# Two wide products, then two narrow ones: the order of a column block's matmuls in a split-precision stream

## The chip, the cores and the metric

The kernel runs on one core of a Trainium2 chip. The metric is the device time in microseconds of one execution: 2563.12 us, the median of three runs that lie between 2562.52 and 2567.24 us.

## The reference

The computation is a small decoder trunk in float32, with one sequence of 256 tokens and a width of 2048. There are two layers. The first mixes tokens with a Mamba-2 state-space block, the second with a short gated convolution. Each is followed by a gated feed-forward network with a convolution of its own (hidden width 5632), and a root-mean-square norm ends it. Nearly all of the arithmetic is in the dense products by weight matrices:

```python
h = rms_norm(x, mix_norm_w[i])
x = x + mixer(h)                      # ssd_mixer (i = 0), short_conv_mixer (i = 1)
h = rms_norm(x, ffn_norm_w[i])
hu = causal_dwconv(h @ w_up, conv_w, conv_b)
g, v = jnp.split(hu, 2, axis=-1)
x = x + (silu(g) * v) @ w_down
...
return rms_norm(x, final_norm_w)
```

## The kernel before

**Split products.** TensorE takes operands in a shortened float32 form (`F32R` in the code), which drops low bits. To get more precise results the kernel splits each operand in two: a high half, which is the value rounded to that form, and a low half, which is what rounding left over. A product of weights and activations is then high by high, plus high weights by low activations, plus low weights by high activations. For the activations both halves lie side by side in one tile `hl`: 256 columns (the tokens) high, 256 columns low. For the weights they are two tiles, `wh` and `wl`.

**Units of weights.** Weights come in units of two blocks of 128 rows (`KU = 2`) by 512 columns. A unit is loaded by one DMA on SyncE's queue into a `raw` tile (line 267; four buffers). ScalarE casts it into `wh` (line 287), and VectorE subtracts to get `wl` (line 288); both have four buffers (`WB = 4`). A plan lists all units in the order of use, and `weight_unit` (line 298) hands out the next one after it has had up to three further ones loaded and split.

**Streams.** `stream` (line 308) multiplies a slice of 512 weight columns with all of an activation. The result, transposed, is 512 rows by 256 tokens, kept as four column blocks `t` of 128 weight columns each, two to a PSUM tile `pts[t // 2]`. For each unit, and in it for each column block `t` and each of the two row blocks `k`, the weights' 128 x 128 block is the stationary operand, and the activation streams past it:

- a *wide* product (line 334): high weights by the whole `hl` row block, 512 columns. The high-by-high sum falls in the first 256 columns of the PSUM tile, the high-by-low sum in the last 256.
- a *narrow* product (line 335): low weights by the high half of `hl`, 256 columns, added to the first 256 columns of the same place.

Each of them needs its own stationary block, so a weight load on TensorE (PEld in the profile) precedes every matmul. The code issues them in the order wide k=0, narrow k=0, wide k=1, narrow k=1, and then takes the next column block. A unit has eight wide and eight narrow products.

Some streams (`one` set: the state-space block's B, C and x inputs) put the high and low activation sums in the same 256 columns. They have two products of 256 columns (lines 331 and 332) in place of the wide one. The very first stream (`before` set) is interleaved by hand with the start of the kernel, and its instructions are kept in the program's order by `put = pin`. All others leave the order to the scheduler: the program's order is the priority, and the scheduler estimates by a simulation of its own when an instruction is ready, and lets a later one go first where it is not.

At the end of a stream `evac` is called for each of the two PSUM tiles: ScalarE and VectorE add the two sums, scale, convolve or add to the residual. There are three such PSUM tiles, so one of the next stream's is free at once.

The last feed-forward's down projection doesn't go through `stream`. It keeps tokens in rows (lines 858 to 860): three products of 512 columns each, with activations as the stationary operand and weights streaming past.

Of the kernel before, what the change touches and what calls it, by code (L numbers as in the profile page):

```python
# [16 lines left out]
P = 128  # L17
T = 256
# [14 lines left out]
KU = 2  # L33
# [6 lines left out]
def trunk_kernel(ctx, tc, a, out):  # L40
    nc = tc.nc
    mm = nc.tensor.matmul
# [18 lines left out]
    def uid(s):  # L61
        n_id[0] += 1
        return f"{s}_{n_id[0]}"
# [11 lines left out]
    start = ExitStack()  # L75
# [49 lines left out]
    for name, r in rows:  # L125
        base[name] = at
        lo = 0
        while lo < r.shape[0]:
            i, off = divmod(at, P)
            n = min(P - off, r.shape[0] - lo)  # L130
# [146 lines left out]
    def load_unit():  # L277
        i = len(units)
        if i == len(raws):
            load_raw()  # L280
        raw, raws[i] = raws[i], None
        wh = wpool.tile([P, KU, COLS], F32R, tag="wh", name=uid("wh"))
        wl = wpool.tile([P, KU, COLS], F32R, tag="wl", name=uid("wl"))
        units.append((wh, wl))

        def half(ks, put):
            put(nc.scalar.copy(wh[:, ks, :], raw[:, ks, :]))  # L287
            put(tt(  # L288
                out=wl[:, ks, :], in0=raw[:, ks, :], in1=wh[:, ks, :].bitcast(F32),
                op=ALU.subtract,  # L290
            ))

        if i == 0:
            return half
        with tc.high_priority(0 if i < NKD // KU else None):
            half(slice(0, KU), pin if i < NKD // KU + 2 else lambda ins: ins)

    def weight_unit(c0, kc, ahead=WB - 1):

        i = taken[0]  # L300
        assert plan[i][1:] == (c0, kc), (plan[i], c0, kc)
        taken[0] += 1
        while len(units) < min(i + ahead + 1, len(plan)):
            load_unit()
        got, units[i] = units[i], None
        return got

    def stream(c0, hls, kcs, evac, one=False, before=None):

        pts = [psm.tile([P, 2, 512], F32, tag="main", name=uid("main")) for _ in range(2)]
        n = len(kcs)
        put = (lambda ins: ins) if before is None else pin
        for u in range(0, n, KU):
            order = [(t, k) for t in range(4) for k in range(KU)]
            if before is not None and u == 0:
                before(0)
                order.sort(key=lambda tk: tk[1])  # L320
            wh, wl = weight_unit(c0, kcs[u], WB - 1 if before is None else 0)
            for at, (t, k) in enumerate(order):
                if before is not None and at == (0 if u else 2) and u + KU < n:
                    before(u // KU + 1)
                i = u + k
                o = pts[t // 2][:, t % 2, :]
                hl = hls[i // 2][:, i % 2, :]
                lw = slice(t * P, (t + 1) * P)
                first, last = i == 0, i == n - 1
                if one:  # L330
                    put(mm(o[:, 0:T], wh[:, k, lw], hl[:, 0:T], start=first, stop=False))  # L331
                    put(mm(o[:, 0:T], wh[:, k, lw], hl[:, T : 2 * T], start=False, stop=False))  # L332
                else:
                    put(mm(o, wh[:, k, lw], hl, start=first, stop=False))  # L334
                put(mm(o[:, 0:T], wl[:, k, lw], hl[:, 0:T], start=False, stop=last))  # L335
        if before is not None:
            before(n // KU)
        if taken[0] < len(plan):
            while len(units) < min(taken[0] + WB - 1, len(plan)):
                load_unit()  # L340
        for p in range(2):
            evac(p, pts[p])
# [62 lines left out]
    first = {}  # L405
# [50 lines left out]
    def bc_stream(g, o, before=None):  # L456

        res = []

        def evac(p, pt):  # L460
            k0 = DI // P + o * NG + g + 2 * p
            s = scaled(pt, first["r0"], True)
            y = conv(s, W_SSD, "ssdw", NCX, k0, "ssdb", "bc", bcpool)
            act(y, y, AF.Silu)
            res.append(y)

        stream(2 * DI + o * NG * DS + g * DS, xhl, range(NKD), evac, True, before)
        return res
# [101 lines left out]
    def xs_stream(g):  # L570
        res = [None, None]

        def evac(p, pt):
            y = conv(scaled(pt, r0, True), W_SSD, "ssdw", NCX, g * 4 + 2 * p, "ssdb", "xs", xspool)
            act(y, y, AF.Silu)
            res[p] = y

        stream(DI + g * GC, xhl, range(NKD), evac, True)
        return res

    def z_stream(g):
        res = [None, None]

        def evac(p, pt):
            q = pair_sum(pt)
            z = pair_tmp("z", sp)
            tt(out=z, in0=q, in1=rep2(r0), op=ALU.mult)
            act(z, z, AF.Silu)
            res[p] = z

        stream(g * GC, xhl, range(NKD), evac)
        return res
# [174 lines left out]
    for part in range(2):  # L767
        hid = ffn_part(0, part, xhl, r)
        last = part == 1
# [43 lines left out]
    for c in range(2):  # L813
        for q in range(4):
            ps = aux()
            for j in range(4):
                k = 4 * q + j
# [22 lines left out]
    for part in range(2):  # L840
        lo, hi = FPARTS[part]
        hid = ffn_part(1, part, xhl, r)
        n = hi - lo
        for cg in range(D // COLS):
# [17 lines left out]
            def evac(c):  # L862
                x = xtok[c][:, cols]
                tt(out=x, in0=pt[:, c, :], in1=x, op=ALU.add)  # L864
                if part == 1:
                    junk = tmp.tile([P, 512], F32, tag="tp", name=uid("tp"))
                    act(junk, x, AF.Square, accum_out=ss[:, c, cg : cg + 1])
                    tt(out=x, in0=x, in1=fin[:, cols], op=ALU.mult)
                if end:
                    finish(c)  # L870
# [42 lines left out]
```

## Time and profile before

| | |
|---|---|
| median of the runs | 2563.12 us |
| the profiled execution's own time | 2563.32 us |
| its span, first to last instruction | 2561.5 us |
| mean granted TensorE clock | 0.998 |
| TensorE matmuls | 15101, busy 99% of the span |
| TensorE weight loads | 15101, busy 87% |
| VectorE, ScalarE | busy 70% and 52% |
| DMA | 478.76 MB, mean 187 GB/s |

The busy time of an engine is the time in which at least one of its instructions is marked as running. TensorE's matmuls overlap in the marks: each is shown from its start to a modelled end, and the next starts before that. The sum of the groups' busy times is therefore larger than the span, and the distance from one matmul's start to the next is what it costs. The rows of the timeline show start, length, engine, line of the kernel, operation, tiles written and read, the shape of the stationary and of the moving operand, and a count of instructions that were merged into the row. In the rows of groups the figure behind the last bar is the time in which the engine stood idle just before such an instruction, and whom it waited for.

### The profile page before, as it was taken

The numbers are of one execution on the slowest core, as the hardware profiler recorded it, in microseconds if no ns is written. First come the engines' busy times: TensorE is split into PE (matmuls) and PEld (weight loads), VectorE is DVE, ScalarE is ACT, GpSimd is POOL, SyncE is SP. The second block draws the span as 40 slices with busy tenths as digits, with TensorE's granted clock in tenths as the row PEclk, the third lists the DMA queues.
The fourth block names the chain that finished last, engine by engine and source line by source line (L and its number), as shares of the span: only waits on it lengthen the run. The fifth ranks groups of instructions, "written<-read, shape, count | busy, mean of one in ns | idle before, by whom it ended". The sixth has DMA issues, their size and how long they took to land.

```text
span 2561.5 us, 38324 instructions
## 1 busy us (share of the span) xinstructions
PE 2544.6 (99%) x15101; PEld 2235.2 (87%) x15101; DVE 1790.2 (70%) x2601; ACT 1321.5 (52%) x1630; POOL 1.1 (0%) x8
## 2 busy tenths in 40 slices
PE   9999999999999999999999999999999999999998
PEld 9999998998888888888888888888888888888886
DVE  7888876788677776557776666666677774577765
ACT  5565643566555554345554444444555553455543
POOL 0000000000000000000000000000000000000000
PEclk9999999999999999999999999999999999999999
DMA  7666655665666665666665666666566666666664
GB/s 229 175 184 193 182 176 188 189 182 172 198 183 191 190 188 181 193 188 183 193 190 181 193 186 185 185 197 189 174 183 187 189 197 190 193 186 188 189 192 145
DMA packets 255737, 478.76 MB, mean 187 GB/s; under 512 B 17668, under 2 KB 29124, under 8 KB 255428
## 3 DMA queue, kind: packets, MB, share of 16 engines
q1 hardware_dynamic: 254643, 474.13, 61.3%
q8 instruction: 118, 1.93, 0.3%
q10 hardware_dynamic: 912, 2.18, 0.2%
q14 instruction: 64, 0.52, 0.1%
HBM read 474.09 MB, written 2.16 MB: 186 GB/s over the span
## 4 chain that ended last, share of the span: by engine, by line
PE 98%; DVE 1%; ACT 1%; DMA 0%; issue 0%; SPq 0%; DVEq 0%; ACTq 0%
PE main L334 50%; PE main L335 29%; PE main L331 3%; PE main L332 3%; PE main L858 3%; PE main L859 3%; PE main L860 3%; PE aux L649 1%; DVE wl L288 0%; PE aux L657 0%; DMA bias_bc<-in_ssd_dt_bias_dram 0%; PE aux L513 0%; PE aux L630 0%; DMA raw<-in_ssd_w_in_dram 0%; ACT wh L287 0%; PE aux L187 0%
## 5 line engine op out<-in xcount | busy, mean ns | idle before, releaser
L334 PE MATMUL main<-hl,wh 128*128 128x512 f32 x5568 | 1944.9, 396 | 0.2 <-DVE hl L218 0.2
L335 PE MATMUL main<-hl,wl 128*128 128x256 f32 x6336 | 1749.2, 281 | 1.8 <-DVE wl L288 1.8
L288 DVE TENSOR_TENSOR wl<-raw,wh 128x1024 fp32r<-128x1024 f32 (+1 forms) x881 | 1072.6, 1221 | 702.2 <-ACT wh L287 701.6
L287 ACT CAST wh<-raw 128x1024 fp32r<-128x1024 f32 (+1 forms) x881 | 920.8, 1048 | 1067.7 <-PE main L334 735.2
L334 PEld LDWEIGHTS main<-hl,wh 128*128 128x128 f32 x5568 | 1034.8, 188 | 236.7 <-issue 2.0
L335 PEld LDWEIGHTS main<-hl,wl 128*128 128x128 f32 x6336 | 1196.9, 189 | 17.6 <-DVE wl L288 2.7
L331 PE MATMUL main<-hl,wh 128*128 128x256 f32 x768 | 219.5, 287 | 2.5 <-DVE tp L354 1.3
L332 PE MATMUL main<-hl,wh 128*128 128x256 f32 x768 | 218.6, 285 | 0.0
L331 PEld LDWEIGHTS main<-hl,wh 128*128 128x128 f32 x768 | 148.2, 193 | 4.0 <-issue 2.0
L332 PEld LDWEIGHTS main<-hl,wh 128*128 128x128 f32 x768 | 148.3, 193 | 1.5 <-issue 1.1
L858 PE MATMUL main<-wh,hl 128*128 128x512 f32 x352 | 137.5, 391 | 0.8 <-DVE xtok L864 0.8
L859 PE MATMUL main<-wl,hl 128*128 128x512 f32 x352 | 137.4, 390 | 0.0
L860 PE MATMUL main<-wh,hl 128*128 128x512 f32 x352 | 137.0, 389 | 0.0
L370 DVE SCALAR_TENSOR_TENSOR tp<-tp,prm,tp 128x255 f32<-128x255 f32 x208 | 90.6, 477 | 0.0
L346 ACT COPY tp<-main 128x512 f32<-128x512 f32 x128 | 74.3, 580 | 26.0 <-PE main L335 26.0
L348 DVE TENSOR_TENSOR tp<-main,tp 128x512 f32<-128x512 f32 x128 | 87.4, 683 | 0.0
L858 PEld LDWEIGHTS main<-wh,hl 128*128 128x128 f32 x352 | 66.1, 188 | 15.3 <-DVE xtok L864 1.2
L860 PEld LDWEIGHTS main<-wh,hl 128*128 128x128 f32 x352 | 66.1, 188 | 14.2
L859 PEld LDWEIGHTS main<-wl,hl 128*128 128x128 f32 x352 | 66.1, 188 | 13.6
L370 DVE SCALAR_TENSOR_TENSOR g<-tp,prm,g 128x254 f32<-128x254 f32 (+1 forms) x176 | 74.6, 477 | 0.1
L368 ACT ACTIVATE g<-tp,prm,prm 128x256 f32<-128x256 f32 x88 | 48.2, 596 | 38.0 <-DVE tp L357 38.0
L357 DVE TENSOR_TENSOR tp<-tp,rrow 128x512 f32<-128x512 f32 x96 | 66.0, 688 | 1.8
(134 smaller groups left out, 966.9 us busy)
## 6 DMA issues: line engine op xcount, KB each, us to landing
raw<-in_ffn_w_up_dram SPq DMA_DIRECT2D x352, 512.0 KB, 3.7
raw<-in_ffn_w_down_dram SPq DMA_DIRECT2D x176, 512.0 KB, 4.1
raw<-in_ssd_w_in_dram SPq DMA_DIRECT2D x159, 512.0 KB, 4.5
raw<-in_sc_w_in_dram SPq DMA_DIRECT2D x96, 512.0 KB, 4.1
raw<-in_ssd_w_out_dram SPq DMA_DIRECT2D x64, 512.0 KB, 4.2
raw<-in_sc_w_out_dram SPq DMA_DIRECT2D x32, 512.0 KB, 4.2
cbc<-cs_d SPq DMA_DIRECT2D x32, 256.0 KB, 5.1
xt<-in_x_dram SPq DMA_DIRECT2D x8, 256.0 KB, 7.4
```

Source lines behind the costliest of these rows:

```text
L287: put(nc.scalar.copy(wh[:, ks, :], raw[:, ks, :]))
L288: put(tt(out=wl[:, ks, :], in0=raw[:, ks, :], in1=wh[:, ks, :].bitcast(F32), op=ALU.subtract,))
L331: put(mm(o[:, 0:T], wh[:, k, lw], hl[:, 0:T], start=first, stop=False))
L332: put(mm(o[:, 0:T], wh[:, k, lw], hl[:, T : 2 * T], start=False, stop=False))
L334: put(mm(o, wh[:, k, lw], hl, start=first, stop=False))
L335: put(mm(o[:, 0:T], wl[:, k, lw], hl[:, 0:T], start=False, stop=last))
L346: nc.scalar.copy(pb, pt[:, :, T : 2 * T])
L348: tt(out=s, in0=pt[:, :, 0:T], in1=pb, op=ALU.add)
L370: stt(out=y[:, j, d:T], in0=s[:, j, 0 : T - d], scalar=pcol(wname, (width - 1 - d) * nk + k0 + j), in1=y[:, j, d:T], op0=ALU.mult, op1=ALU ...
L858: mm(pt[:, c, :], hi_, wh[:, k, :], start=(i == 0), stop=False)
L859: mm(pt[:, c, :], hi_, wl[:, k, :], start=False, stop=False)
L860: mm(pt[:, c, :], lo_, wh[:, k, :], start=False, stop=(i == n - 1))
```

## The change

Within a unit, a column block now issues the products of both row blocks with the high weights first, and then both with the low weights: wide k=0, wide k=1, narrow k=0, narrow k=1. For streams with `one` set it is four products by high weights and then the two by low weights. The narrow product becomes a small function `low`. The first stream keeps the old order. Number, operands and flags of the matmuls are the same, with the accumulation's `stop` on the last narrow product as before, and the scheduler still has the last word on the order. The last down projection is not touched.

```diff
             wh, wl = weight_unit(c0, kcs[u], WB - 1 if before is None else 0)
+
+            def low(t, k):
+                i = u + k
+                put(mm(
+                    pts[t // 2][:, t % 2, 0:T], wl[:, k, t * P : (t + 1) * P],
+                    hls[i // 2][:, i % 2, 0:T], start=False, stop=(i == n - 1),
+                ))
+
             for at, (t, k) in enumerate(order):
...
-                first, last = i == 0, i == n - 1
+                first = i == 0
                 if one:
                     put(mm(o[:, 0:T], wh[:, k, lw], hl[:, 0:T], start=first, stop=False))
                     put(mm(o[:, 0:T], wh[:, k, lw], hl[:, T : 2 * T], start=False, stop=False))
                 else:
                     put(mm(o, wh[:, k, lw], hl, start=first, stop=False))
-                put(mm(o[:, 0:T], wl[:, k, lw], hl[:, 0:T], start=False, stop=last))
+                if before is not None:
+                    low(t, k)
+                elif k == KU - 1:
+                    for q in range(KU):
+                        low(t, q)
```

## The prediction

> **What bounds the kernel now.** I read the page first: the busy table, the chain of waits, the groups. Then the waits of TensorE alone, and last the order and distance of its instructions in time, since the change is one of order.
>
> ```profile
> span 2561.5 us, 38324 instructions
> PE 2544.6 (99%) x15101; PEld 2235.2 (87%) x15101; DVE 1790.2 (70%) x2601; ACT 1321.5 (52%) x1630; POOL 1.1 (0%) x8
> PE 98%; DVE 1%; ACT 1%; DMA 0%; issue 0%; SPq 0%; DVEq 0%; ACTq 0%
> L334 PE MATMUL main<-hl,wh 128*128 128x512 f32 x5568 | 1944.9, 396 | 0.2 <-DVE hl L218 0.2
> L335 PE MATMUL main<-hl,wl 128*128 128x256 f32 x6336 | 1749.2, 281 | 1.8 <-DVE wl L288 1.8
> L287 ACT CAST wh<-raw 128x1024 fp32r<-128x1024 f32 (+1 forms) x881 | 920.8, 1048 | 1067.7 <-PE main L334 735.2
> L288 DVE TENSOR_TENSOR wl<-raw,wh 128x1024 fp32r<-128x1024 f32 (+1 forms) x881 | 1072.6, 1221 | 702.2 <-ACT wh L287 701.6
> L334 PEld LDWEIGHTS main<-hl,wh 128*128 128x128 f32 x5568 | 1034.8, 188 | 236.7 <-issue 2.0
> ```
>
> The chain is TensorE for 98% of the span, and its idle time at the two lines is 2.0 us in all. ScalarE and VectorE, which split the weights, stand idle for over 700 us each while TensorE is behind. So the time is the sum of the distances between matmul starts, and only that matters here. The durations of 396 and 281 ns are no use for it: one pair of them is 677 ns, and the next pair starts after half of that. I take distances from start to start.
>
> ```profile
> L334 PE MATMUL main<-hl,wh 128*128 128x512 f32 x3925 | 1367.8, 396 | 0.0
> L335 PE MATMUL main<-hl,wl 128*128 128x256 f32 x3924 | 1080.6, 280 | 0.0
> L818 PE MATMUL aux<-ident,x 128*128 128x128 f32 x32 | 4.3, 272 | 0.0
> ```
>
> These are the groups of TensorE in the stretch from 700 to 2080 us, which is nothing but wide-narrow streams and some 56 small matmuls. 1380 us less about 6 us for those, by 3925 pairs, is 0.350 us for a wide and a narrow product. Two pairs, which is what the change reorders, take 0.700 us.
>
> **The distance isn't one number.** Here are two stretches of strict alternation, each by its first and last wide product (from the timeline) and the row that counts them.
>
> ```profile
> 361.64 0.40 PE L335 MATMUL main<-hl,wl 128*128 128x256 f32 x2
> 361.88 0.40 PE L334 MATMUL main<-hl,wh 128*128 128x512 f32 x1
> ...
> 374.71 0.39 PE L334 MATMUL main<-hl,wh 128*128 128x512 f32 x1
> L334 PE MATMUL main<-hl,wh x38: 392/394/400, 361.9 to 374.7; 128*128 128x512 f32 x38
> ...
> 384.32 0.40 PE L335 MATMUL main<-hl,wl 128*128 128x256 f32 x2
> 384.56 0.40 PE L334 MATMUL main<-hl,wh 128*128 128x512 f32 x1
> ...
> 397.63 0.40 PE L334 MATMUL main<-hl,wh 128*128 128x512 f32 x1
> L334 PE MATMUL main<-hl,wh x38: 395/398/403, 384.6 to 397.6; 128*128 128x512 f32 x38
> ```
>
> 38 starts are 37 distances. The first stretch gives 12.83 / 37 = 0.3468 us a pair, the second 13.07 / 37 = 0.3532, with the same instructions in the same order and no idle time. TensorE holds one step or the other for dozens of pairs. Two pairs cost 0.6935 in the fast step and 0.7065 in the slow one; the mean of 0.700 is about half of each. What flips it is seen where the order is broken, since the scheduler already leaves strict alternation at some unit boundaries:
>
> ```profile
> 1210.19 0.28 PE L335 MATMUL main<-hl,wl 128*128 128x256 f32 x1
> 1210.31 0.62 PE L334 MATMUL main<-hl,wh 128*128 128x512 f32 x2
> 1210.77 0.28 PE L335 MATMUL main<-hl,wl 128*128 128x256 f32 x1
> ...
> 1211.23 0.40 PE L334 MATMUL main<-hl,wh 128*128 128x512 f32 x1
> 1211.47 0.28 PE L335 MATMUL main<-hl,wl 128*128 128x256 f32 x1
> ...
> 1212.29 0.40 PE L334 MATMUL main<-hl,wh 128*128 128x512 f32 x1
> ...
> 1213.24 0.40 PE L335 MATMUL main<-hl,wl 128*128 128x256 f32 x2
> 1213.47 0.40 PE L334 MATMUL main<-hl,wh 128*128 128x512 f32 x1
> 1213.71 0.28 PE L335 MATMUL main<-hl,wl 128*128 128x256 f32 x1
> ```
>
> Two wide products in a row take 0.46 us (1210.31 to 1210.77), and the three pairs from 1211.23 to 1212.29 take 1.06 us, which is the slow step of 0.353. Two narrow ones in a row take 0.23 us (1213.24 to 1213.47), and the wide one behind them 0.24 us. A doubled product by itself costs nothing that shows, but it changes the step that follows. The change puts one at every place.
>
> **The change part by part.** No instruction is added or taken away, no DMA moves, and nothing passes another queue. In the 5568 wide products of line 334, all in streams that the change touches, two and two become a group of wide, wide, narrow, narrow: 5568 / 2 = 2784 groups. Each nanosecond of a group is 2.8 us of the kernel.
>
> *The group.* Of its four distances two are of a kind that before hardly has (wide to wide, narrow to narrow), and two stay (wide to narrow, narrow to wide). For the new kind I use stretches of one width alone.
>
> ```profile
> L858 PE MATMUL main<-wh,hl x59: 389/389/392, 2160.2 to 2199.8; 128*128 128x512 f32 x59
> ...
> 310.50 0.28 PE L332 MATMUL main<-hl,wh 128*128 128x256 f32 x1
> 310.62 0.28 PE L335 MATMUL main<-hl,wl 128*128 128x256 f32 x1
> 310.74 0.28 PE L331 MATMUL main<-hl,wh 128*128 128x256 f32 x1
> 310.86 0.28 PE L332 MATMUL main<-hl,wh 128*128 128x256 f32 x1
> ```
>
> In the last down projection, wide products alone, line 858 comes once in three matmuls: 39.6 us / 58 / 3 = 0.2276 us for one. In a stream whose moving side is narrow throughout, each takes 0.120 us. Both load new weights for every matmul. Two of each are 2 x 0.2276 + 2 x 0.120 = 0.6952 us. The bounds: 0.6935 below, the fast step, since no long stretch of the trace is under it (the doubled rows would add to 0.46 + 0.23 = 0.69, but a start is only marked to 10 ns there, and the next distances are longer); 0.7065 above, the slow step. I take half from the unmixed rows and half from the alternation, as two of four distances change their kind: (0.6952 + 0.700) / 2 = 0.6976. That is 2.4 ns less than now, x 2784 = 6.7 us gained. By the bounds it would be 18 us gained or 18 us lost.
>
> *The narrow-only streams.* The 768 blocks of lines 331 and 332, of which the first stream's 64 keep their order, have three matmuls of 256 columns each, 0.120 us in every order in the rows above: nothing.
>
> *Waits.* The narrow products read the low half of the weights, which VectorE writes last; the first of a unit now comes one wide product (0.23 us) later.
>
> ```profile
> PE main L335 <- DVE wl L288: 1.8, 3, 1.4
> ```
>
> Three waits, each shortened by 0.23 us at most, and the longest may lie in the first stream, which is left as it was: 0 to 0.7 us gained, I take 0.3. The last wide product of a unit comes 0.12 us earlier, so the buffer of the high half is free for ScalarE's cast that much sooner. It is worth nothing: cast and subtraction are 1048 + 1221 ns, one behind the other, and a unit of eight pairs lasts 8 x 0.350 = 2.8 us; if they ever ran short, 0.12 us a unit is what this would give. The last product of each block is still a narrow one at the same place, so the evacuations start as before. The waits of the weight-load queue that are an instruction of their own stay about as many:
>
> ```profile
> L334 PEldq EVENT_SEMAPHORE  x24: 51/51/51, 373.2 to 1814.4; - x24
> ```
>
> 24 x 51 ns is 1.2 us; none of them or twice as many would be 1.2 us either way. I take no change.
>
> **The sum.** The profiled execution took 2563.3 us beside its span of 2561.5, and lies 0.2 us over the median of 2563.12. 2563.3 - 6.7 - 0.3 = 2556.3; I say 2556 us.
>
> **The rivals.**
>
> *The order is indifferent: 2563 us.* If a distance goes by the width of the matmul itself and not by its neighbour, a group costs the same 0.700 in any order. For it: the doubled rows (0.23 for a wide, 0.115 for a narrow) are the alternating ones to within their 10 ns. Against it: the two steps show that the same width can take more or less time. Here belongs also that the order stays as it was, because the scheduler puts instructions where it estimates them ready; the new order is the program's order and nothing in it waits longer, so I give that little. TensorE's page of the Trainium skill (TensorE: Matmul & The Clock Gate, Back-to-back issue gap) has the columns by 2.4 plus 2.5 ns for one matmul, whatever its neighbour. Its estimate for a group, 650 ns, lies well under the 700 of the trace, so some 50 ns of each group are not in that rule.
>
> *All of the slow step goes: 2545 us.* If a doubled product at every place holds TensorE in the fast step, a group is 0.6935: 6.5 ns x 2784 = 18 us. For it: behind the doubled narrow product at 361.64 the fast step begins and lasts for 37 pairs. Against it: behind the doubled narrow product at 384.32 the slow one does.
>
> *Slower: the slow step holds, 2581 us.* Place: the weight load under the second narrow product.
>
> ```profile
> 1200.14 0.27 PE L335 MATMUL main<-hl,wl 128*128 128x256 f32 x1
> 1200.14 0.19 PEld L334 LDWEIGHTS main<-hl,wh 128*128 128x128 f32 x1
> 1200.25 0.40 PE L334 MATMUL main<-hl,wh 128*128 128x512 f32 x1
> ```
>
> A load is marked 188 ns and starts with the matmul before it, and a narrow product gives it only 0.115 to 0.120 us before the next must start. Now a wide product behind each narrow one gives the chain room again; in the new order two such loads follow one another, and a lateness of the first is handed to the second. Above 0.700 a group the kernel is slower, above 0.702 by more than the 5 us that can be measured (5 us / 2784); at the slow step, 0.7065, it costs 6.5 ns x 2784 = 18 us. For it: behind the doubled narrow product at 1213.24 the wide one takes 0.24, and behind the doubled wide one at 1210.31 the slow step begins. Against it: narrow products in an endless row keep 0.120 with a load under each. The Trainium skill speaks for this rival (the same page, LDWEIGHTS): a load is its columns by 1.2, some 107 ns as an estimate, so that a narrow product covers it with almost nothing to spare. The trace agrees in so far as the unmixed narrow rows never go under it.
>
> **How the numbers follow.** The forecast (2550 to 2558) has 0.38, the slow step gone 0.13, indifferent 0.23, slower 0.26. A measurement of this kernel can tell about 0.2%, 5 us, from no change. Of the forecast's 0.38 I count 0.32 as faster by more and 0.06 as the same; of the indifferent 0.23, 0.01 falls on each side. Faster: 0.32 + 0.13 + 0.01 = 0.46; same: 0.06 + 0.21 = 0.27; slower: 0.26 + 0.01 = 0.27. The range reaches from 2541 (all of the slow step gone, and the waits) to 2581 (the slow step held): what is left out is some 0.15, mostly above, where a mixed order could be dearer than either step. The likeliest case's own range is 2550 to 2558.
>
> **What would show it.** In the timeline of the changed kernel, in a steady stretch, lines for the wide and the narrow products stand two and two; the starts of every second wide product are 0.698 apart (0.6935 to 0.7065 by the rivals). Lengths that flip between two steps as now would show that the steps stay. Idle time of TensorE at the narrow line should be at most 1.8 us. The idle time of ScalarE behind the wide line should change by no more than the span does. I am wrong in the mechanism if TensorE's idle time grows by more than 5 us, if the chain shows another engine with more than its 1%, or if a group settles on a distance that neither step nor the unmixed rows have.

## The result, and the profile after

The changed kernel takes 2550.59 us (median of four runs, 2550.41 to 2551.46), against 2562.82 us before: a ratio of 0.9949 with a 95% interval of 0.9932 to 0.9966. That is 12.2 us or 0.5% faster. Run a second time beside other kernels it gave 0.9951 (0.9939 to 0.9964).

The page of the changed kernel: span, busy table, chain by engine, and the groups of the two lines. The wide product is line 342 now, the narrow one line 325, and the last down projection lines 870 to 872.

```profile
span 2548.6 us, 38320 instructions
PE 2531.2 (99%) x15101; PEld 2227.1 (87%) x15101; DVE 1792.8 (70%) x2601; ACT 1312.5 (51%) x1622; POOL 1.1 (0%) x8
PE 98%; DVE 1%; DMA 0%; ACT 0%; issue 0%; SPq 0%; DVEq 0%
L342 PE MATMUL main<-hl,wh 128*128 128x512 f32 x5568 | 1747.6, 396 | 0.8 <-DVE hl L218 0.8
L325 PE MATMUL main<-hl,wl 128*128 128x256 f32 x6336 | 1253.5, 279 | 1.7 <-DVE wl L288 1.7
L287 ACT CAST wh<-raw 128x1024 fp32r<-128x1024 f32 (+1 forms) x881 | 922.3, 1049 | 1066.5 <-PE main L342 707.3
```

The number of matmuls is as before, the engines' shares and the chain are so to within one per cent, and the mean of a wide product is the same 396 ns. The groups' busy times fell (line 342 shows 1747.6 us where line 334 showed 1944.9), but that is only because neighbours of one line now overlap in the marks. What fell is the distance from start to start, and with it the span, by 12.9 us. Here is the timeline in a steady stretch (the last figure of a row is the number of instructions merged into it):

```profile
1300.18 0.63 PE L342 MATMUL main<-hl,wh 128*128 128x512 f32 x2
1300.65 0.39 PE L325 MATMUL main<-hl,wl 128*128 128x256 f32 x2
1300.88 0.62 PE L342 MATMUL main<-hl,wh 128*128 128x512 f32 x2
1301.34 0.40 PE L325 MATMUL main<-hl,wl 128*128 128x256 f32 x2
1301.57 0.63 PE L342 MATMUL main<-hl,wh 128*128 128x512 f32 x2
1302.04 0.39 PE L325 MATMUL main<-hl,wl 128*128 128x256 f32 x2
1302.27 0.62 PE L342 MATMUL main<-hl,wh 128*128 128x512 f32 x2
1302.73 0.40 PE L325 MATMUL main<-hl,wl 128*128 128x256 f32 x2
1302.97 0.40 PE L342 MATMUL main<-hl,wh 128*128 128x512 f32 x1
```

The scheduler issues what the program says. Four groups take 1302.97 - 1300.18 = 2.79 us, 0.6975 each by marks of 10 ns. For a finer figure I count the wide products in the stretch from 700 to 2070 us: of before first, then of the changed kernel.

```profile
L334 PE MATMUL main<-hl,wh 128*128 128x512 f32 x3896 | 1357.7, 396 | 0.0
```

```profile
L342 PE MATMUL main<-hl,wh 128*128 128x512 f32 x3917 | 1229.5, 395 | 0.0
```

1370 us less some 6 us for the small matmuls is 0.3501 us a pair before and 0.3482 us after, so 0.7002 and 0.6965 for a group of two and two. The 3.7 ns between them, times 2784 groups, are 10.3 us. The stretch from the first wide product to the last says the same. Of before, and of after:

```profile
L334 PE MATMUL main<-hl,wh x5568: 387/395/504, 94.5 to 2440.5; 128*128 128x512 f32 x199
```

```profile
L342 PE MATMUL main<-hl,wh x5568: 387/396/499, 92.4 to 2427.4; 128*128 128x512 f32 x199
```

It shrank from 2346.0 to 2335.0 us, by 11.0 us. The other 2 us of the two spans lie ahead of the first wide product (94.5 against 92.4). There the first stream keeps its old order, but the narrow-only streams behind it have the new one. In the profiles of the kernels whose narrow-only streams have the old order this point lies at 92.9 to 94.5 us, in those with the new order at 92.1 to 93.6, so I count the 2 us as mostly scatter of single profiles.

### The profile page after: what moved, and what is told of

Same layout as the page of the kernel before. It is cut to its first block, busy times and chain, and to the rows that moved or that the text cites. A ratio compares the mean times of both kernels' runs of the same rounds, so it can differ in the third digit from the quotient of the medians.

```text
span 2548.6 us, 38320 instructions
## 1 busy us (share of the span) xinstructions
PE 2531.2 (99%) x15101; PEld 2227.1 (87%) x15101; DVE 1792.8 (70%) x2601; ACT 1312.5 (51%) x1622; POOL 1.1 (0%) x8
## 4 chain that ended last, share of the span: by engine, by line
PE 98%; DVE 1%; DMA 0%; ACT 0%; issue 0%; SPq 0%; DVEq 0%
PE main L342 51%; PE main L325 29%; PE main L339 4%; PE main L340 4%; PE main L870 3%; PE main L871 3%; PE main L872 3%; PE aux L661 1%; DMA cbc<-cs_d 0%; PE aux L669 0%; PE aux L525 0%; PE aux L642 0%; PE aux L187 0%; PE warm L96 0%; DMA raw<-in_ssd_w_in_dram 0%; PE aux L433 0%
## 5 line engine op out<-in xcount | busy, mean ns | idle before, releaser
L342 PE MATMUL main<-hl,wh 128*128 128x512 f32 x5568 | 1747.6, 396 | 0.8 <-DVE hl L218 0.8
L287 ACT CAST wh<-raw 128x1024 fp32r<-128x1024 f32 (+1 forms) x881 | 922.3, 1049 | 1066.5 <-PE main L342 707.3
L325 PEld LDWEIGHTS main<-hl,wl 128*128 128x128 f32 x6336 | 1162.6, 188 | 246.8 <-issue 3.3
L325 PE MATMUL main<-hl,wl 128*128 128x256 f32 x6336 | 1253.5, 279 | 1.7 <-DVE wl L288 1.7
L342 PEld LDWEIGHTS main<-hl,wh 128*128 128x128 f32 x5568 | 852.1, 189 | 5.4 <-DVE hl L218 1.0
L339 PE MATMUL main<-hl,wh 128*128 128x256 f32 x768 | 204.3, 286 | 2.5 <-DVE tp L366 1.3
L340 PE MATMUL main<-hl,wh 128*128 128x256 f32 x768 | 203.0, 284 | 0.1
L339 PEld LDWEIGHTS main<-hl,wh 128*128 128x128 f32 x768 | 147.8, 192 | 3.5 <-issue 2.1
L340 PEld LDWEIGHTS main<-hl,wh 128*128 128x128 f32 x768 | 147.9, 193 | 0.7 <-issue 0.4
```

The lines of the kernel that those rows point to most:

```text
L325: put(mm(pts[t // 2][:, t % 2, 0:T], wl[:, k, t * P : (t + 1) * P], hls[i // 2][:, i % 2, 0:T], start=False, stop=(i == n - 1),))
```

## The experiments

Four theories appear in the expectations. A: the kind of neighbour sets a distance, so that more neighbours of one kind make it cheaper. B: what costs is irregularity, and any regular order is good. C: it counts whether neighbours add to the same place in PSUM. D: each repeating order settles on a step of its own, which isn't a sum over neighbours. D was formed after the first four runs. The diffs are shortened. Two runs of the old order (the first and the last below) edit the kernel before, all others the changed kernel. `W` stands for a wide product and `n` for a narrow one.

**The old order, kept regular within a unit.**

```diff
-                    put(mm(o, wh[:, k, lw], hl, start=first, stop=False))
-                put(mm(o[:, 0:T], wl[:, k, lw], hl[:, 0:T], start=False, stop=last))
+                    (pin if at else put)(mm(o, wh[:, k, lw], hl, start=first, stop=False))
+                (put if one else pin)(mm(o[:, 0:T], wl[:, k, lw], ..., stop=last))
```

> The old order (wide, narrow, wide, narrow), but within a unit every wide and narrow product is held in the program's order, so that the scheduler leaves no doubled product inside a unit. Theory A (the kind of neighbour sets the distance; alternation costs 0.700 us for two pairs on the mean): nothing changes, 2563 us within 3. Theory B (the irregular places throw TensorE into the slow step, and regular alternation stays in one step for good): the two steps no longer mix; 2545 us if it is the fast one (0.6935 for two pairs), 2581 us if it is the slow one (0.7065), and one of them in nearly all of the stretch from 700 to 2080 us.

Measured: a ratio of 1.0005 (0.9996 to 1.0014), no difference; 2565.1 us beside 2563.7. In the stretch from 1300 to 1800 us it has 1424 wide products, and before has 1426:

```profile
L334 PE MATMUL main<-hl,wh 128*128 128x512 f32 x1424 | 498.4, 396 | 0.0
```

Both steps are still there, in somewhat longer stretches: by the starts in the two traces up to 83 pairs in one step, where before has up to 73. Breaks were left between units and streams. So regularity inside a unit is worth nothing, and the run doesn't decide between A and B for an order without breaks.

**The new order, turned by one place:** `W n n W` in each block, so that the doubled wide products fall across two blocks.

```diff
-                    high(t, 0); high(t, 1); low(t, 0); low(t, 1)
+                    high(t, 0); low(t, 0); low(t, 1); high(t, 1)
```

> The changed order turned by one place: wide k=0, narrow k=0, narrow k=1, wide k=1, so that the doubled wide products fall across two column blocks, or two units, and no longer go to the same place in PSUM. The sequence of widths is the changed kernel's, shifted. If widths alone set the distance (theories A and B): a group takes 0.6965 us as in the changed kernel, and the time is 2551 us within 3. If it counts that two wide products add to the same place in PSUM (theory C): the group goes back towards 0.700 and the time towards 2560 us.

Measured: a ratio of 0.9982 (0.9973 to 0.9991), 2559.5 us. By the time alone that looks like theory C. The timeline says otherwise:

```profile
1304.27 0.62 PE L340 MATMUL main<-hl,wh 128*128 128x512 f32 x2
...
1309.84 0.40 PE L340 MATMUL main<-hl,wh 128*128 128x512 f32 x1
```

Between these two rows lie eight groups, so one takes 5.57 / 8 = 0.696 us, as in the changed kernel, though its doubled wide products add to two different places. In the stretch from 1300 to 1800 us, this kernel and the changed one each have 1434 wide products:

```profile
L340 PE MATMUL main<-hl,wh 128*128 128x512 f32 x1434 | 451.0, 395 | 0.0
```

```profile
L342 PE MATMUL main<-hl,wh 128*128 128x512 f32 x1434 | 449.6, 395 | 0.0
```

Theory C falls. The run also speaks against a rival that wasn't named. In the changed kernel no two neighbours read the same activations; here, as in alternation, a wide product and the narrow one of the same row block `k` stand side by side and do. A group costs the same all the same. The lost time lies in the transitions: comparing the starts of wide products of equal number in the two traces, this kernel falls 7.2 us behind the changed one between the first wide product and 641 us (by the changed kernel's time), 4.9 us of it from 616 to 641, where the first feed-forward network begins, and only 0.4 us in all the rest. One wait of 1.8 us of TensorE for that network's activations is part of it. Why the scheduler's order comes out dearer there I didn't follow up.

**All eight wide products of a unit, then its eight narrow ones.**

```diff
-                for t in range(4): (wide k=0, wide k=1, narrow k=0, narrow k=1)
+                for t in range(4): wide k=0, wide k=1
+                for t in range(4): narrow k=0, narrow k=1
```

> All eight wide products of a unit (in the narrow-only streams all sixteen by high weights), then its eight narrow ones. Theory A: of sixteen distances only two join unlike widths, so the unit comes to the sum of the unmixed rows, 8 x 0.2276 + 8 x 0.120 = 2.781 us, 0.695 for two and two, some 1.3 ns under the changed kernel's group: 2547 us within 3. Theory B (only the regularity counts): between the fast and the slow step, no forecast nearer than 2545 to 2560 us. Slower than 2563 us would mean that a run of narrow products does expose weight loads.

Measured: a ratio of 0.9994 (0.9985 to 1.0002), 2562.6 us: no gain. A stretch of eight and eight in its timeline:

```profile
1308.98 1.11 PE L325 MATMUL main<-hl,wl 128*128 128x256 f32 x8
1309.93 2.00 PE L340 MATMUL main<-hl,wh 128*128 128x512 f32 x8
1311.77 1.00 PE L325 MATMUL main<-hl,wl 128*128 128x256 f32 x7
```

Eight narrow products take 0.95 us, 0.119 each, as in the unmixed rows. Eight wide ones take 1.84 us, 0.230 each, where the unmixed row had 0.2276. Together it is 2.79 us a unit, 0.698 for two and two: dearer than the changed kernel's 0.6965, though it has far fewer junctions of unlike kinds. It isn't the rounding of one stretch: the median of all 349 repetitions of eight and eight in the trace is 0.698. Theory A falls with this.

The starts in the traces, which are marked to 1 ns, show where the time goes. Here are the distances behind each product, as means over the uninterrupted repetitions:

| order | behind the wide products, ns | behind the narrow products, ns |
|---|---|---|
| alternating (before) | 234 | 116 |
| two and two (the change) | 233, 233 | 115, 116 |
| eight and eight | 233, 236, 229, 232, 230, 227, 227, 227 | 113, 119, 120, 120, 120, 120, 120, 120 |

A wide product comes down to the 227 ns of the unmixed rows only behind five others, and a narrow one costs less than the unmixed 120 ns only near a wide one. So the neighbours do count, but over several places, and with opposite signs for the two widths.

The scheduler also made stretches of four and four out of this program, which took more still; the run of four and four below tests them by themselves.

**Which streams hold the gain.** The change in the wide streams alone, and in the narrow-only streams alone:

```diff
-                if before is not None:
+                if before is not None or one:        # wide streams only
+                if before is not None or not one:    # narrow-only streams only
                     low(t, k)
```

> The change only in the streams with wide products; those with 256 columns alone keep the old order. All theories that put the gain into the wide and narrow distances: 2551 us within 2. If a part of the gain comes from the narrow-only streams, or from the different schedule of the first 100 us, it is that much slower: 2553 us or more.

> The change only in the narrow-only streams; the wide and narrow products alternate as before. If the gain is all in the wide and narrow distances: 2563 us within 1.5. If the narrow-only streams, or the schedule around them in the first 600 us, hold a part of it: 2559 to 2561.5 us, and together with the run of the wide streams alone it adds up to the changed kernel.

> The changed kernel once more, beside the next one on the same chip, to part the wide streams from the rest. All theories: 2550.6 us within 2.

Measured: 0.9957 (0.9945 to 0.9970), 2552.4 us, with the wide streams alone; 1.0001 (0.9993 to 1.0010), 2563.9 us, with the narrow-only streams alone; 2551.6 us for the whole change, 12.3 us under the narrow-only run of the same chip. All of the gain that can be told from no change is in the wide streams. The first and the last wide product of the whole change and of the narrow-only run:

```profile
L342 PE MATMUL main<-hl,wh x5568: 387/396/499, 92.9 to 2428.6; 128*128 128x512 f32 x199
```

```profile
L342 PE MATMUL main<-hl,wh x5568: 387/395/504, 92.6 to 2439.2; 128*128 128x512 f32 x199
```

Here both start together, and the stretch is 2335.7 against 2346.6 us: 10.9 us again, of which 10.3 is the groups.

**Four and four.**

```diff
+                for t in (0, 2):
+                    for j in range(2 * KU): high(t + j // KU, j % KU)
+                    for j in range(2 * KU): low(t + j // KU, j % KU)
```

> Two column blocks taken together: four wide products, then four narrow ones (the narrow-only streams as in the changed kernel). Theory A (the kind of neighbour sets the distance, so longer runs are cheaper): 0.696 us for two and two, 2549 us or less. Theory D (each repeating pattern settles on a step of its own, which isn't the sum of its neighbours): the stretches of four and four that stood in the run with eight and eight took 1.405 us, 0.7025 for two and two, 6 ns over the changed kernel's 0.6965; x 2784 = 17 us over the changed kernel, 2567 us and so slower than before.

Measured: a ratio of 0.9998 (0.9989 to 1.0007), 2563.7 us.

```profile
1302.68 1.09 PE L340 MATMUL main<-hl,wh 128*128 128x512 f32 x4
1303.61 0.64 PE L325 MATMUL main<-hl,wl 128*128 128x256 f32 x4
1304.09 1.09 PE L340 MATMUL main<-hl,wh 128*128 128x512 f32 x4
...
1309.70 0.63 PE L340 MATMUL main<-hl,wh 128*128 128x512 f32 x2
```

From the first row to the last there are five repetitions: 7.02 / 5 = 1.404 us, 0.702 for two and two. Theory D's step for four and four stands, if a little lower: over all 1182 repetitions in the trace the mean is 0.701. The expectation took 0.7025, and the 1.2 to 1.4 ns between them, times 2784, come to the 3 to 4 us by which the time is better than it said. All gain over the alternation is lost, with half as many junctions of unlike kinds as in the changed kernel.

**Three and three, three and three, two and two.**

```diff
+                tk = [(t, k) for t in range(4) for k in range(KU)]
+                for part in (tk[0:3], tk[3:6], tk[6:8]):
+                    (the wide products of part, then its narrow ones)
```

> A unit's eight wide and eight narrow products as three and three, three and three, two and two. Theory A: between the changed kernel and the unmixed rows, 2550 us within 2. Theory D: a step of its own, between the floor of 0.6935 and the slow step's 0.7065 for two and two (2543 to 2580 us), the same in all steady stretches.

Measured: a ratio of 0.9987 (0.9979 to 0.9996), 2560.9 us. In the stretch from 1300 to 1800 us there are 1430 wide products where alternation had 1426 and the changed kernel 1434. Theory A's 2550 is out of reach. Theory D's forecast holds: by the starts in the trace, 357 of its 373 repetitions take 0.699 or 0.700 for two and two, a step of its own.

**Part of the blocks doubled:** the new order in the first of a unit's four blocks, or in every second one.

```diff
+                    if t == 0:        # or: t % 2 == 0
+                        high(t, 0); high(t, 1); low(t, 0); low(t, 1)
+                    else:
+                        high(t, 0); low(t, 0); high(t, 1); low(t, 1)
```

> The new order in the first of a unit's four column blocks, alternation in the other three; a repeating pattern of sixteen matmuls. Theory D: one step of its own in all steady stretches, between 0.6935 and 0.7065 us for two and two (2543 to 2580 us). If the gain were in proportion to the doubled places: a quarter of it, 2560 us.

> The new order in every second column block, alternation in the others; a repeating pattern of eight matmuls. Theory D: one step of its own, between 0.6935 and 0.7065 us for two and two (2543 to 2580 us). In proportion to the doubled places: half the gain, 2557 us.

Measured: 1.0000 (0.9991 to 1.0009), 2563.8 us, and 1.0011 (1.0002 to 1.0020), 2566.6 us. Half of the change doesn't bring half of the gain: it brings none, and if anything a loss. With every second block doubled, two groups repeat like this:

```profile
705.47 0.62 PE L340 MATMUL main<-hl,wh 128*128 128x512 f32 x2
705.93 0.40 PE L325 MATMUL main<-hl,wl 128*128 128x256 f32 x2
706.17 0.40 PE L340 MATMUL main<-hl,wh 128*128 128x512 f32 x1
706.40 0.28 PE L325 MATMUL main<-hl,wl 128*128 128x256 f32 x1
706.52 0.40 PE L340 MATMUL main<-hl,wh 128*128 128x512 f32 x1
706.76 0.28 PE L325 MATMUL main<-hl,wl 128*128 128x256 f32 x1
706.88 0.62 PE L340 MATMUL main<-hl,wh 128*128 128x512 f32 x2
```

That is 1.41 us, 0.705 by marks of 10 ns; the mean of the 1091 such repetitions in the trace is 0.703. With the first block doubled, the order has two steps again, like the alternation that makes up most of it. Two of its units:

```profile
1011.48 0.63 PE L340 MATMUL main<-hl,wh 128*128 128x512 f32 x2
1014.29 0.62 PE L340 MATMUL main<-hl,wh 128*128 128x512 f32 x2
...
1305.92 0.63 PE L340 MATMUL main<-hl,wh 128*128 128x512 f32 x2
1308.70 0.85 PE L340 MATMUL main<-hl,wh 128*128 128x512 f32 x3
```

The unit that begins at 1011.48 takes 2.81 us, the one at 1305.92 takes 2.78 us. So the part of theory D that gave each order one step alone is wrong for it. Theory B falls too: four and four, three and three with two and two, and every second block doubled are all regular, and none of them is as good as two and two.

**Alternation without breaks.** The old order, held strictly from the first feed-forward network to the last down projection.

```diff
-        put = (lambda ins: ins) if before is None else pin
+        put = pin if before is not None or held[0] else (lambda ins: ins)
...
     mixer.close()
+    held[0] = True
```

> The old order, and from the first feed-forward network to the last down projection every matmul of a stream is held strictly in the program's order, so that alternation is broken only where a stream waits for PSUM and by the few small matmuls of the norms. Theory D (alternation has two steps and keeps the one it is in until something breaks it): stretches of one step over many streams, 0.6935 or 0.7065 us for two pairs and nothing between. Held in the fast step throughout it would save some 5 ns x 2400 groups of that part, 2550 us; held in the slow one, 2578 us; waits that the fixed order brings at the start of a stream come on top. If the step still changes within unbroken stretches, theory D is wrong for alternation.

Measured: a ratio of 1.0161 (1.0147 to 1.0175), 2604.7 us. Most of the loss of 41 us has its own cause, named beforehand (waits that the fixed order brings) but not priced. The norms' small matmuls can't be hidden behind the next stream any more:

```profile
L187 PE MATMUL aux<-dg,ones 128*128 128x128 f32 x15 | 4.4, 424 | 8.2 <-DVE dg L179 8.2
L194 PE MATMUL aux<-ones,nacc 128*128 128x1 f32 x12 | 3.0, 357 | 18.7 <-DVE nacc L397 18.7
1471.00:1479.00 8.00, 4.99 (x17) 4.46 (x18) 3.07 (x16) 0.37 (x1) 0.00 (x0) 0.50 0.02 7
```

TensorE stands idle there for 18.7 + 8.2 = 26.9 us, and around one such wait the granted clock (the third figure from the end of the last row) is 0.50 over 8 us. What the run was for is seen in the stretch in front of it:

```profile
L336 PE MATMUL main<-hl,wh x759: 392/395/515, 728.3 to 991.2; 128*128 128x512 f32 x190
L336 PE MATMUL main<-hl,wh x94: 391/398/403, 991.9 to 1024.8; 128*128 128x512 f32 x94
L336 PE MATMUL main<-hl,wh x489: 392/395/395, 1130.8 to 1300.0; 128*128 128x512 f32 x163
```

758 distances in 262.9 us are 0.3468 us a pair, the fast step through many streams; before, without this, held it for dozens of pairs. Then, from about 992 us on, 93 distances take 32.9 us, 0.354 each. At that point no matmul is out of order and none waits in the timeline. Later, in the last row, 488 distances take 169.2 us, 0.3467 each: the fast step again. So an unbroken order holds a step for long, with nothing between the two, but not for good. By the words of the expectation theory D is wrong for alternation, and what ends a step I can't name. What is left of D is that a repeating order's cost has to be measured on that order.

## Why the prediction was right or wrong

**The bound and the place of the gain were right.** The sum of distances between matmul starts is the time; TensorE is 98% of the chain as before. Its idle time at the narrow line went from 1.8 to 1.7 us, where a fall of 0.3 us was forecast; the waits of the weight-load queue stayed at 24. The narrow-only streams were worth nothing, as said. The scheduler kept the new order, so that rival falls. One sign came out otherwise: ScalarE's idle time behind the wide line fell from 735.2 to 707.3 us, by 27.9 us and so by more than the span. Its idle time before the casts as a whole went from 1067.7 to 1066.5, so most of the difference was put down to other engines, and TensorE's own waits for the weights stayed as they were.

**The group's term had the right sign and the wrong size.** The step was the price of 0.6976 us for two and two, half from the rows of one width alone and half from the alternation. Measured is 0.6965, a gain of 3.7 ns and not 2.4 in each group, 10.3 us and not 6.7. (By the starts of the uninterrupted groups alone it is 0.7000 and 0.6966, 3.4 ns and 9.5 us.) With that the measured 2550.6 us lies at the lower edge of the forecast's own 2550 to 2558. Some 2 to 3 us of the measured 12.2 us are outside of what the groups account for, and I can't place them.

**The reasoning behind that price was wrong.** It took each distance as the property of a matmul and its neighbour. The unmixed rows gave 0.6952 for two and two, so a longer run of one width should have come nearer to it. Eight and eight gave 0.698 and four and four 0.702. In the changed kernel the two wide products cost 5 to 6 ns more each than the unmixed rows, and the two narrow ones 4 to 5 ns less; that the half-and-half price came near the measured one is luck. The prediction had named its own sign of this: it would be wrong in the mechanism if a group settled on a distance that neither step nor the unmixed rows have. 0.6965 is such a distance. Right, and more useful, was the reading just ahead of the price: TensorE holds one step or another for the same instructions, and the step changes where the order is broken. Of the 134 unbroken alternations of twelve pairs or more in the trace of before, 130 keep one step to their end; the other four, and the run without breaks, show that a step can also end by itself. From there the prediction should have said that the cost of a new repeating order can't be had from the pieces of an old one.

**The rivals.** Indifferent order is refuted for the whole change (0.9949), though several other orders happen to cost the same as alternation. All of the slow step gone would be 0.6935; the changed kernel stays 3 ns a group above it. (The range's lower end of 2541 is a slip of some 2 us: 2563.3 less 18 and less the two terms for waits, 0.7 and 1.2, is 2543.4.) The slower rival priced the load under the second of two narrow products; in the changed kernel the distances behind its two narrow products are 0.115 and 0.116 us, less than the unmixed 0.120, and in runs of eight each takes 0.119, so the price isn't paid. Slower orders do exist, but not by that mechanism: 0.702 with four and four.

## What to carry to other kernels

When TensorE is the bound and matmuls of two widths alternate, the order of widths is worth a try by itself: here it moved the same four matmuls from 0.700 us on the mean to 0.6965 at best and 0.703 at worst. Price it by running the whole repeating order, not by adding distances of neighbours from another order; a partial or a longer version of a good order may bring nothing. And measure the distance from start to start over a counted stretch, since the mean marked duration of a wide product stayed at 394 to 397 ns in every run.

## What the runs showed of the hardware that was not expected

The same four matmuls, two wide and two narrow, with a weight load under each and no idle time, take in steady stretches (the granted clock is 0.997 to 0.999 on the mean of each of these kernels):

| order | us for two and two |
|---|---|
| alternating, fast step | 0.6935 |
| two and two (the change) | 0.6965 |
| eight and eight | 0.698 |
| three and three, three and three, two and two | 0.699 |
| four and four | 0.702 |
| every second block doubled | 0.703 |
| alternating, slow step | 0.7065 |

Alternation has two steps, and in an unbroken order it kept the fast one for 263 us. Whether the two wide products of a group add to one place in PSUM or to two makes no difference (two and two, turned by one place: 0.696). A wide product's distance falls from 233 to 236 ns to 227 only along a run of six, and a narrow one's rises from 113 to 120 ns within three. What in TensorE makes these steps stays open: no run here looks inside it.
